# Last rows of a decoder block: final factor, gain and row sum applied by VectorE in place of GpSimd, and one more block of a modulation sum on TensorE

## The chip, the cores and the metric

The kernel runs on one core of one Trainium2 chip. The metric is the device time of one execution in microseconds (us). A core has five engines that run side by side and meet through semaphores: TensorE (PE in the profile, its weight loads PEld), VectorE (DVE), ScalarE (ACT), GpSimd (POOL) and SyncE (SP), which here only issues DMAs.

## What is computed

One layer of a decoder trunk on 512 rows of width 1024, all in float32: an adaLN-modulated RMSNorm, two attention mixers, a gated convolutional MLP, and a final RMSNorm. The two places that the change touches are the first modulation and the last norm:

```python
mod = cs @ w_ada[l] + b_ada[l]                  # cs = silu(c), 1024 long
shift1, scale1, gate1, shift2, scale2, gate2 = jnp.split(mod, 6, axis=-1)
h = _rmsnorm(x, norm1_g[l]) * (1.0 + scale1) + shift1
...
x = x + gate2 * _conv_ffn(h2, ...)
return _rmsnorm(x, final_g)                     # y = x * rsqrt(mean(x*x) + eps) * g
```

## The kernel before, in words

**The whole.** 128 rows or columns make a block. Every fp32 product is made of three matmuls of split values (high times high, high times low, low times high), and TensorE works nearly without a pause from the first projection to the last product. Most of the order of work is written out by hand: inside `tc.manual_schedule` an engine takes its instructions in the order in which the code names them. SyncE's order at the end follows from what it waits for.

**The start.** The first block of columns of the modulation needs two sums over the eight blocks `kk` of `c`: `j = 0` is the scale, `j = 1` the shift. Each is shared between two engines. TensorE multiplies the first `DIRECT[j]` blocks of weights directly with `cs` (`direct0`, L451). VectorE adds the other blocks up in the tile `a0[j]` with one instruction for a block (`add_a0`, L445 for the first, L447 for each further one), and TensorE then sums `a0[j]` over its partitions with a matrix of ones and adds it to the same bank (L475). `finish_mod` (L333 scale, L339 shift) makes the factors, `h_tile` (L383, ScalarE) applies them to the transposed `x` in bank `xt`, and with that the first projection matmul (L403) can run. `turn(t)` (L432) puts the block of rows `t` of `x` into that bank. A float32 matmul appears as two entries ("passes") in the profile, a transpose as one.

**The end.** The last two blocks of rows, 2 and 3 (`u = 0, 1`), get their last product in `last_rows`: all 512 columns of `u = 0`, then columns 0 to 255 (`c0`) and 256 to 511 (`c1`) of `u = 1`, the last piece into a bank of its own (`dX`). From there on only the other engines work. The first half of the 1024 output columns is still to be finished: `last_mul` (L1883) multiplies the bank by the gate, `last_sum` (L1886) adds it to `x`, `last_square` (L1891, ScalarE) squares it and sums each row, `root` (L1903) takes the root, `root_inverse` (L1908, L1910) inverts it, and `rstd_end` (L201, L205) refines it into the row factor `rs`. Meanwhile GpSimd multiplies the new `x` by the final gain `fgb` into `m1` (`last_gain`, L1895; the profile calls the tile `pairs`), and VectorE multiplies that by `rs` (`last_scale`, L1914). The second half of the columns already holds `x` times gain in `e2` (the profile's `chain_outl`) and needs only `rs` (`last_scale2`: VectorE, L1922, for `u = 0`; ScalarE, L1920, for `u = 1`). Each piece is sent out with its own DMA: `u = 0` in two pieces of 256 KB, `u = 1` in four of 128 KB, seven of the eight output DMAs on SyncE's queue (`finished` at L1943 sends rows 0 and 1) and one on ScalarE's.

Of the kernel before, what the change touches and what calls it, by code (L numbers as in the profile page):

```python
# [10 lines left out]
AF = mybir.ActivationFunctionType  # L11
ALU = mybir.AluOpType
PSUM = bass.MemoryType.PSUM

P = 128
D = 1024
S = 512
KT = D // P
# [42 lines left out]
def kernel(  # L61
# [22 lines left out]
    nc = tc.nc  # L84
    xd, wada, win, wout, wup, wdown = x[0], w_ada[0], w_in[0], w_out[0], w_up[0], w_down[0]
    wba, wbd, od = w_branch_swa[0], w_branch_diff[0], out[0]

    def pool(name, bufs=1, space=None, stack=ctx):
        kw = {} if space is None else {"space": space}
        return stack.enter_context(tc.tile_pool(name=name, bufs=bufs, reuse_waits="tile", **kw))  # L90
# [107 lines left out]
    def rstd_end(dst, ms, r0, n, wpool):  # L198
        t = wpool.tile([P, n], F32, tag="rs_b", bufs=3, name="rt")
        if n == 1:  # L200
            nc.vector.scalar_tensor_tensor(t, r0, r0, ms, ALU.mult, ALU.mult)  # L201
        else:
            nc.vector.tensor_mul(t, r0, r0)
            nc.vector.tensor_mul(t, t, ms)
        nc.vector.scalar_tensor_tensor(dst, t, -3.0, r0, ALU.add, ALU.mult)  # L205
# [124 lines left out]
    def finish_mod(k, pa):  # L330
        pa = pa if k == 0 else [pa[:, 0], pa[:, 1]]
        m = pp.tile([P, 16], F32, tag="mod", bufs=3, name=f"mod{k}")
        last = nc.vector.scalar_tensor_tensor(  # L333
            m[:, 0:1], pa[0][:, 0:1], bsc1[:, k : k + 1], n1g[:, k : k + 1], ALU.add, ALU.mult
        )
        if k:
            nc.scalar.activation(m[:, 1:2], pa[1][:, 0:1], AF.Identity, bias=bsh[:, k : k + 1])
        else:
            nc.vector.tensor_add(m[:, 1:2], pa[1][:, 0:1], bsh[:, k : k + 1])  # L339
        mods[k] = m  # L340
        return last
# [12 lines left out]
    def split_hi(k, part=None):  # L354
        if part != 1:
            pl, nb = (wp, WB) if k % 2 == 0 else (pp, 2)
            wh = pl.tile([P, 768], F32R, tag="whi", bufs=nb, name=f"w0h{k}")
            wl = pl.tile([P, 768], F32R, tag="wlo", bufs=nb, name=f"w0l{k}")
            wts[k] = (wh, wl)
            rq, wq, lq = w0_views(k)  # L360
            nc.scalar.copy(wq, rq)
        if part != 0:
            nc.scalar.copy(wts[k][0][:, 512:768], w0[k][:, 512:768])
# [55 lines left out]
    def root(t):  # L419
        rstd_end(rst[:, t : t + 1], *half[t], 1, pp)  # L420
# [10 lines left out]
    def turn(t):  # L431
        nc.tensor.transpose(pts[0][:, t * P : (t + 1) * P], xn[:, t, 0:P], ident)  # L432

    def scale_x(t):
        nc.scalar.activation(xn[:, t, HEAD:], xn[:, t, HEAD:], AF.Copy, scale=rst[:, t : t + 1])

    pa0 = [tbank("pa0", (P, P)), acc6[4][:, :P]]
    a0 = [pp.tile([P, P], F32, name=f"a0_{j}") for j in range(2)]
    DIRECT = (5, 4)

    def add_a0(j, kks):
        for kk in kks:
            w, f = adaw[0][:, j, kk], cs[:, kk : kk + 1]
            if kk == DIRECT[j]:
                nc.vector.tensor_scalar_mul(a0[j], w, f)  # L445
            else:
                nc.vector.scalar_tensor_tensor(a0[j], w, f, a0[j], ALU.mult, ALU.add)  # L447

    def direct0(j):
        for kk in range(DIRECT[j]):  # L450
            nc.tensor.matmul(  # L451
                pa0[j], adaw[0][:, j, kk], cs[:, kk : kk + 1].to_broadcast([P, P]), start=kk == 0, stop=False
            )

    for t in range(NT):
        stat(t)
        if t in (1, 2):
            normalise(t - 1)
            turn(t - 1)
            keep_warm((4, 1)[t - 1])  # L460
    root(2)
    add_a0(0, range(DIRECT[0], KT - 1))
    root(3)
    add_a0(0, range(KT - 1, KT))
    add_a0(1, range(DIRECT[1], KT))
    scale_x(0)
    scale_head(2)
    scale_head(3)
    scale_x(1)
    direct0(0)  # L470
    turn(2)
    direct0(1)
    turn(3)
    for j in range(2):
        nc.tensor.matmul(pa0[j], a0[j], ones, start=False, stop=True)  # L475
    finish_mod(0, pa0)
    split_hi(0, 0)
    keep_warm(2)
# [616 lines left out]
    bp = pool("mlp")  # L1095
# [134 lines left out]
    for h in range(2):  # L1230
        c1 = 2 * P
# [237 lines left out]
    def ks(g):  # L1469
        return slice(2 * (g % 2), 2 * (g % 2) + 2)  # L1470
# [25 lines left out]
    V, q0, q1 = nc.vector, ks(0), ks(1)  # L1496
# [81 lines left out]
    fgb = bp.tile([P, D], F32, tag="fgb", name="fgbr")  # L1578
# [167 lines left out]
    s2 = big.tile([P, NPR, H], F32, tag="hhA", name="s2")  # L1746
# [3 lines left out]
    m1 = pairs2.rearrange("p (t n) -> p t n", n=S)  # L1750
    e = cbuf[1][:, 1024:2048].rearrange("p (t n) -> p t n", n=S)
    e2 = cbuf[3][:, 1024:2048].rearrange("p (t n) -> p t n", n=S)
# [61 lines left out]
    def stat_end(t):  # L1814
        rs = bp.tile([P, 1], F32, tag="rs2", bufs=4, name=f"rsd{t}")
        rstd_end(rs, *parts[t], 1, bp)
        return rs

    def res(t, hf):
        return x1[:, t, hf * S : (hf + 1) * S]  # L1820
# [61 lines left out]
    def last_mul(u, sl=slice(0, S), bank=dW):  # L1882
        nc.vector.tensor_mul(m1[:, u, sl], bank[u][:, sl], gate(0)[:, sl])  # L1883

    def last_sum(u, sl=slice(0, S)):
        nc.vector.tensor_add(res(2 + u, 0)[:, sl], res(2 + u, 0)[:, sl], m1[:, u, sl])  # L1886

    def last_square(u, sl=slice(0, S)):
        sq = big.tile([P, S], F32, tag="sq2", name=f"sqe{u}_{sl.start}")
        s1 = bp.tile([P, 1], F32, tag="ss2", bufs=8, name=f"sse{u}_{sl.start}")  # L1890
        nc.scalar.activation(sq[:, sl], res(2 + u, 0)[:, sl], AF.Square, accum_out=s1)  # L1891
        return s1

    def last_gain(u, sl=slice(0, S)):
        nc.gpsimd.tensor_tensor(m1[:, u, sl], res(2 + u, 0)[:, sl], fgb[:, sl], ALU.mult)  # L1895

    def partial(s1, plus=EPS):
        nc.vector.tensor_scalar(s1, s1, 1.0 / D, plus, ALU.mult, ALU.add)
        return s1
# [3 lines left out]
        nc.scalar.activation(q, s1, AF.Sqrt, bias=plus, scale=1.0 / D)  # L1903
        return q

    def root_inverse(s1, q, plus):
        ms = bp.tile([P, 1], F32, tag="rs_a", bufs=3, name="ms")
        nc.vector.scalar_tensor_tensor(ms, s1, 1.0 / D, plus, ALU.mult, ALU.add)  # L1908
        r0 = bp.tile([P, 1], F32, tag="rs_c", bufs=3, name="r0")
        nc.vector.reciprocal(r0, q)  # L1910
        return ms, r0

    def last_scale(u, rs, sl=slice(0, S)):
        nc.vector.tensor_scalar_mul(res(2 + u, 0)[:, sl], m1[:, u, sl], rs)  # L1914
        nc.sync.dma_start(od[(2 + u) * P : (3 + u) * P, sl], res(2 + u, 0)[:, sl])

    def last_scale2(u, rs, sl=slice(0, S), q=nc.sync):
        dst, src = res(2 + u, 1)[:, sl], e2[:, u, sl]
        if u:
            nc.scalar.activation(dst, src, AF.Copy, scale=rs)  # L1920
        else:
            nc.vector.tensor_scalar_mul(dst, src, rs)  # L1922
        q.dma_start(od[(2 + u) * P : (3 + u) * P, S + sl.start : S + sl.stop], dst)

    def last_rows(todo):
        man = ExitStack()
        man.enter_context(
            tc.manual_schedule(engines={nc.vector.engine, nc.scalar.engine, nc.tensor.engine, nc.gpsimd.engine})
        )
        c0, c1 = slice(0, H), slice(H, S)  # L1930
        part = [partial(parts[2 + u, 1]) for u in range(2)]
        for g in todo:
            multiply(len(passes) - 1, g, 0)

        for g in todo:
            multiply(len(passes) - 1, g, 1, c0)
        for g in todo:
            multiply(len(passes) - 1, g, 1, c1, dX, g == todo[0])
        ends = [stat_end(u) for u in range(2)]

        def finished(u):
            nc.scalar.activation(x1[:, u], x1[:, u], AF.Copy, scale=ends[u])
            nc.sync.dma_start(od[u * P : (u + 1) * P, :], x1[:, u])  # L1943

        finished(0)
        last_mul(0)
        last_sum(0)
        s0 = last_square(0)
        q0 = root(s0, part[0])
        finished(1)  # L1950
        last_gain(0)
        last_mul(1)
        h0 = root_inverse(s0, q0, part[0])
        last_sum(1)
        s1 = last_square(1, c0)
        last_gain(1, c0)
        rs0 = bp.tile([P, 1], F32, tag="rs2", bufs=4, name="rse0")
        rstd_end(rs0, *h0, 1, bp)
        last_mul(1, c1, dX)
        last_sum(1, c1)  # L1960
        s2 = last_square(1, c1)
        last_gain(1, c1)
        partial(s1, part[1])
        q1 = root(s2, s1)
        last_scale(0, rs0)
        last_scale2(0, rs0)
        h1 = root_inverse(s2, q1, s1)
        rs1 = bp.tile([P, 1], F32, tag="rs2", bufs=4, name="rse1")
        rstd_end(rs1, *h1, 1, bp)
        for c in (c0, c1):  # L1970
            last_scale(1, rs1, c)
        for c, q in ((c0, nc.sync), (c1, nc.scalar)):
            last_scale2(1, rs1, c, q)
        man.close()

    ops = {}
# [83 lines left out]
```

## Time and profile before

| | |
|---|---|
| median of 3 runs | 686.99 us (686.57 to 687.71) |
| the profiled execution, its own time | 686.37 us |
| its span in the profile | 684.6 us, so 1.8 us lie outside the span |
| TensorE busy | 674.2 us (98% of the span) |
| VectorE, ScalarE, GpSimd busy | 564.6, 383.4, 102.1 us |
| the chain that ended last | TensorE 97%, DMA 1%, VectorE 1% |

In the timeline each row gives the start, the duration, the engine, the line and the operation, the tiles (out<-in) with their sizes, how many instructions are merged (x2), and in brackets how long the engine stood idle before it and who released it. A letter q behind an engine (SPq, ACTq) marks its DMA issues. Times count from the start of the span.

### The profile page before, as it was taken

The page shows a single profiled execution, that of the slowest core. Times are in us where ns is not written, and L with a number is a line of the kernel's source. Part 1 is how long each engine was busy: PE and PEld are TensorE (multiplying, and loading weights), DVE is VectorE, ACT ScalarE, POOL GpSimd, SP SyncE. Part 2 cuts the span into 40 slices and gives each one's busy share as a digit, 9 for nine tenths or more (in the row PEclk, how much of TensorE's full clock was granted, in tenths as well). Part 3 has the DMA queues.
Part 4 walks back from the last instruction along what each step waited for, and adds up shares of the span by engine and source line. Part 5 has one row for each costly group of instructions (what it writes and reads, how often), then busy time and mean ns, then how long its engine had stood idle before and what let it go on. Part 6 is the DMA issues. An engine that isn't in the chain of part 4 may idle for free.

```text
span 684.6 us, 11125 instructions
## 1 busy us (share of the span) xinstructions
PE 674.2 (98%) x4139; PEld 589.3 (86%) x4139; DVE 564.6 (82%) x1076; ACT 383.4 (56%) x687; POOL 102.1 (15%) x122
## 2 busy tenths in 40 slices
PE   8999999999999999999999999999999999999995
PEld 5887887878888888888899999999999998888884
DVE  5999875988796656884689988888888999979997
ACT  6776774546543233324387665565556565656764
POOL 3000000021012012030030210011121003440301
PEclk9999999999999999999999999999999999999998
DMA  9995412565456785669555788777888648995803
GB/s 307 355 302 176 132 62 76 163 165 156 149 150 190 220 255 172 203 175 334 180 101 108 171 207 214 183 168 204 205 208 212 146 169 198 189 205 143 159 0 123
DMA packets 117286, 123.89 MB, mean 181 GB/s; under 512 B 5079, under 2 KB 94456, under 8 KB 117232
## 3 DMA queue, kind: packets, MB, share of 16 engines
q1 hardware_dynamic: 97390, 95.25, 43.5%
q0 software_dynamic: 19648, 27.79, 24.3%
q8 instruction: 32, 0.52, 0.3%
q14 instruction: 22, 0.18, 0.1%
q10 hardware_dynamic: 194, 0.14, 0.1%
HBM read 118.97 MB, written 2.11 MB: 177 GB/s over the span
## 4 chain that ended last, share of the span: by engine, by line
PE 97%; DMA 1%; DVE 1%; SPq 0%; ACT 0%; issue 0%
PE up L1362 32%; PE dc L2004 15%; PE a L403 5%; PE pga L132 2%; PE pga L134 2%; PE pgd L132 2%; PE pgd L133 2%; PE pga L133 2%; PE pgd L134 2%; PE oc L1419 2%; PE oc L1418 2%; PE oc L1422 2%; PE sd L139 1%; PE pq L132 1%; DMA adaw<-in_w_ada_dram 1%; PE pw L132 1%
## 5 line engine op out<-in xcount | busy, mean ns | idle before, releaser
L1362 PE MATMUL up<-t,m_whi 128*128 128x256 f32 x512 | 93.1, 283 | 0.0
L1362 PEld LDWEIGHTS up<-t,m_whi 128*128 128x128 f32 x512 | 79.9, 192 | 0.0
L1362 PE MATMUL up<-t,m_wlo 128*128 128x256 f32 x256 | 72.4, 283 | 0.0
L1362 PE MATMUL up<-bh,p_whi 128*128 128x256 f32 x232 | 65.7, 283 | 0.0
L1362 PE MATMUL up<-bl,p_whi 128*128 128x256 f32 x232 | 65.7, 283 | 0.0
L1362 PE MATMUL up<-bh,p_wlo 128*128 128x256 f32 x232 | 65.7, 283 | 0.0
L952 POOL DMA_DIRECT2D arow<-arow x28 | 22.5, 803 | 245.2 <-DVE sd L821 123.1
L1362 PEld LDWEIGHTS up<-t,m_wlo 128*128 128x128 f32 x256 | 49.2, 192 | 0.0
L1271 POOL DMA_DIRECT2D s<-in_w_up_dram x21 | 27.2, 1371 | 140.9 <-DMA s<-in_w_up_dram 76.2
L1362 PEld LDWEIGHTS up<-bh,p_whi 128*128 128x128 f32 x232 | 44.5, 192 | 0.0
L1362 PEld LDWEIGHTS up<-bl,p_whi 128*128 128x128 f32 x232 | 44.5, 192 | 0.0
L1362 PEld LDWEIGHTS up<-bh,p_wlo 128*128 128x128 f32 x232 | 44.5, 192 | 0.0
L944 DVE SCALAR_TENSOR_TENSOR arow<-ra,cs,arow 128x512 f32<-128x512 f32 x56 | 41.8, 747 | 0.6
L1299 ACT CAST m_whi<-s 128x1024 fp32r<-128x1024 f32 x31 | 32.5, 1047 | 11.1 <-DVE s L1293 7.7
L1303 DVE TENSOR_TENSOR m_wlo<-s,m_whi 128x1024 fp32r<-128x1024 f32 x31 | 37.8, 1218 | 0.0
L1362 PE MATMUL up<-t,p_whi 128*128 128x256 f32 x176 | 32.2, 283 | 0.0
L1362 PEld LDWEIGHTS up<-t,p_whi 128*128 128x128 f32 x176 | 27.5, 192 | 0.0
L816 ACT ACTIVATE sd<-sd,dmx 128x128 f32<-128x128 f32 (+3 forms) x32 | 17.7, 556 | 17.3 <-DVE dmx L806 17.3
L1369 ACT ACTIVATE gT<-a,cv 128x512 f32<-128x512 f32 x22 | 17.7, 814 | 16.9 <-DVE a L1404 15.8
L1299 ACT CAST p_whi<-wa 128x1024 fp32r<-128x1024 f32 x18 | 18.8, 1042 | 12.3 <-PE up L1362 10.5
L1303 DVE TENSOR_TENSOR p_wlo<-wa,p_whi 128x1024 fp32r<-128x1024 f32 x18 | 22.0, 1221 | 3.8 <-ACT p_whi L1299 3.2
L1362 PE MATMUL up<-t,p_wlo 128*128 128x256 f32 x88 | 24.9, 283 | 0.0
(501 smaller groups left out, 2053.9 us busy)
## 6 DMA issues: line engine op xcount, KB each, us to landing
ra<-in_w_ada_dram SPq DMA_DIRECT2D x32, 512.0 KB, 4.9
wa<-in_w_up_dram SPq DMA_DIRECT2D x22, 512.0 KB, 4.9
s<-in_w_up_dram SPq DMA_DIRECT2D x21, 512.0 KB, 4.9
s<-in_w_up_dram POOLq DMA_DIRECT2D x21, 512.0 KB, 6.9
w<-in_w_in_dram SPq DMA_DIRECT2D x12, 512.0 KB, 4.9
a<-in_w_up_dram SPq DMA_DIRECT2D x11, 512.0 KB, 4.8
b<-in_w_down_dram SPq DMA_DIRECT2D x10, 512.0 KB, 4.0
adaw<-in_w_ada_dram SPq DMA_DIRECT2D x8, 512.0 KB, 6.6
```

The lines of the kernel that those rows point to most:

```text
L132: nc.tensor.matmul(o, lh, rh, start=start, stop=False)
L133: nc.tensor.matmul(o, lh, rl, start=False, stop=False)
L134: nc.tensor.matmul(o, ll, rh, start=False, stop=stop)
L403: nc.tensor.matmul(acc6[i], lhs[:, i * P : (i + 1) * P], rhs[k], start=k == 0 and p == 0, stop=last and p == 2)
L816: exp = nc.scalar.activation(pm[m], pm[m], AF.Exp, bias=mx[:, m : m + 1], scale=slope, accum_out=ls)
L944: nc.vector.scalar_tensor_tensor(ac, r[:, a], cc, ac, ALU.mult, ALU.add)
L952: nc.gpsimd.dma_start(whole[0:n], whole[n : 2 * n], accum_op=ALU.add)
L1271: nc.gpsimd.dma_start(dst, upblock(*blk), accum_op=ALU.add)
L1299: nc.scalar.copy(W[J, name][0], R[J, SRC[name]])
L1303: nc.vector.tensor_sub(lo, R[J, SRC[name]], hi.bitcast(F32))
L1362: nc.tensor.matmul(o[u], w[:, k, cu], b[:, k], start=name in ("p1", "m5", "p2") and k == 0 and x == 0, stop=k == 3 and x == 2, skip_group_ ...
L2004: nc.tensor.matmul(bank2[u][:, sl], a[:, q, cu], b[:, q, sl], start=first_mm and x == 0, stop=last_mm and x == 2, skip_group_check=name no ...
```

## The change

At the start both sums now give TensorE five blocks, and VectorE adds three for the shift where it added four. The transpose of the last block of rows of `x` (`turn(3)`) now stands behind the two matmuls that add `a0`, not ahead of them.

At the end GpSimd's multiplication by the gain is gone. VectorE's `scale_first` applies row factor and gain in one instruction of two tensors and one factor, in place. `last_sum(1)` is cut into `c0` and `c1`, with the reciprocal of `u = 0` between the two. The second half of the columns is scaled by ScalarE for both blocks: for `u = 0` in two pieces, one ahead of the last square and one behind the last root, for `u = 1` in one piece of 512. The second halves go out as one DMA each, `u = 1` on ScalarE's queue, so that there are seven output DMAs.

```diff
-    DIRECT = (5, 4)
+    DIRECT = 5
...
     direct0(0)
     turn(2)
     direct0(1)
-    turn(3)
     for j in range(2):
         nc.tensor.matmul(pa0[j], a0[j], ones, start=False, stop=True)
+    turn(3)
     finish_mod(0, pa0)
...
-    def last_gain(u, sl=slice(0, S)):
-        nc.gpsimd.tensor_tensor(m1[:, u, sl], res(2 + u, 0)[:, sl], fgb[:, sl], ALU.mult)
...
+    def scale_first(u, rs, sl=slice(0, S)):
+        x = res(2 + u, 0)[:, sl]
+        nc.vector.scalar_tensor_tensor(x, x, rs, fgb[:, sl], ALU.mult, ALU.mult)
+        nc.sync.dma_start(od[(2 + u) * P : (3 + u) * P, sl], x)
+
+    def scale_second(u, rs, sl=slice(0, S)):
+        nc.scalar.activation(res(2 + u, 1)[:, sl], e2[:, u, sl], AF.Copy, scale=rs)
+
+    def send_second(u, q):
+        q.dma_start(od[(2 + u) * P : (3 + u) * P, S:], res(2 + u, 1))
...
         finished(1)
-        last_gain(0)
         last_mul(1)
-        h0 = root_inverse(s0, q0, part[0])
-        last_sum(1)
+        ms0 = mean(s0, part[0])
+        last_sum(1, c0)
         s1 = last_square(1, c0)
-        last_gain(1, c0)
+        r0 = inverse(q0)
+        last_sum(1, c1)
         rs0 = bp.tile([P, 1], F32, tag="rs2", bufs=4, name="rse0")
-        rstd_end(rs0, *h0, 1, bp)
+        rstd_end(rs0, ms0, r0, 1, bp)
         last_mul(1, c1, dX)
         last_sum(1, c1)
+        scale_second(0, rs0, c0)
         s2 = last_square(1, c1)
-        last_gain(1, c1)
         partial(s1, part[1])
         q1 = root(s2, s1)
-        last_scale(0, rs0)
-        last_scale2(0, rs0)
-        h1 = root_inverse(s2, q1, s1)
+        scale_first(0, rs0)
+        scale_second(0, rs0, c1)
+        send_second(0, nc.sync)
+        ms1 = mean(s2, s1)
         rs1 = bp.tile([P, 1], F32, tag="rs2", bufs=4, name="rse1")
-        rstd_end(rs1, *h1, 1, bp)
+        rstd_end(rs1, ms1, inverse(q1), 1, bp)
         for c in (c0, c1):
-            last_scale(1, rs1, c)
-        for c, q in ((c0, nc.sync), (c1, nc.scalar)):
-            last_scale2(1, rs1, c, q)
+            scale_first(1, rs1, c)
+        scale_second(1, rs1)
+        send_second(1, nc.scalar)
```

`mean` and `inverse` are the two halves of the old `root_inverse`. Lines that start with a minus are of the kernel before, with a plus of the changed one.

TensorE at the start, from the scale's direct matmuls (`pa`) over the shift's (`a_111`) to the warm-up matmul that follows; `xt` is the bank of transposed `x`:

```order
 L451 MATMUL pa_206<-cs,adaw_130 128x128 x5
 L432 MATMUL xt_205<-ident,xn 128x128
-L451 MATMUL a_111<-cs,adaw_130 128x128 x4
+L451 MATMUL a_111<-cs,adaw_130 128x128 x5
+L474 MATMUL pa_206<-ones,a_0_207 128x128
+L474 MATMUL a_111<-ones,a_1_208 128x128
 L432 MATMUL xt_205<-ident,xn 128x128
-L475 MATMUL pa_206<-ones,a_0_207 128x128
-L475 MATMUL a_111<-ones,a_1_208 128x128
 L184 MATMUL a_113<-ones 128x256
```

The shift gets a fifth direct matmul, and the last transpose has moved behind both sums of `a0`.

VectorE at the end, between the gate multiplication of `u = 1` and that of its last piece; `ms`, `r`, `rt` and `rse` are the steps of the row factor of `u = 0`:

```order
-L1908 SCALAR_TENSOR_TENSOR ms<-sse_0_7145,ssd_7022 128x1
-L1910 RECIPROCAL r_7155<-root 128x1
-L1886 TENSOR_TENSOR x_3151<-x_3151,pairs_3623 128x512
-L201 SCALAR_TENSOR_TENSOR rt<-r_7155,ms 128x1
-L205 SCALAR_TENSOR_TENSOR rse_7162<-rt,r_7155 128x1
+L1905 SCALAR_TENSOR_TENSOR ms<-sse_0_7145,ssd_7022 128x1
+L1886 TENSOR_TENSOR x_3151<-x_3151,pairs_3623 128x256
+L1910 RECIPROCAL r_7158<-root 128x1
+L1886 TENSOR_TENSOR x_3151<-x_3151,pairs_3623 128x256
+L201 SCALAR_TENSOR_TENSOR rt<-r_7158,ms 128x1
+L205 SCALAR_TENSOR_TENSOR rse_7161<-rt,r_7158 128x1
```

The addition of 512 columns has become two of 256 with the reciprocal between them.

VectorE a little later, from the last piece's addition to the reciprocal of `u = 1`:

```order
 L1886 TENSOR_TENSOR x_3151<-x_3151,pairs_3623 128x256
-L1898 TENSOR_SCALAR sse_0_7159<-sse_0_7159,ssd_7026 128x1
-L1914 TENSOR_SCALAR x_3151<-pairs_3623,rse_7162 128x512
-L1922 TENSOR_SCALAR x_3151<-chain_outl,rse_7162 128x512
-L1908 SCALAR_TENSOR_TENSOR ms<-sse_256_7169,sse_0_7159 128x1
+L1895 TENSOR_SCALAR sse_0_7156<-sse_0_7156,ssd_7026 128x1
+L1915 SCALAR_TENSOR_TENSOR x_3151<-x_3151,rse_7161,fgbr 128x512
+L1905 SCALAR_TENSOR_TENSOR ms<-sse_256_7169,sse_0_7156 128x1
 L1910 RECIPROCAL r_7181<-root 128x1
```

Where two passes of 512 columns stood ahead of the factor of `u = 1`, there is now one, and it reads two tensors.

More of the change, by code (lines that the diff above doesn't have):

```diff
@@ L443, in add_a0 @@
             w, f = adaw[0][:, j, kk], cs[:, kk : kk + 1]
-            if kk == DIRECT[j]:
+            if kk == DIRECT:
                 nc.vector.tensor_scalar_mul(a0[j], w, f)
@@ L449, in direct0 @@
     def direct0(j):
-        for kk in range(DIRECT[j]):
+        for kk in range(DIRECT):
             nc.tensor.matmul(
@@ L461 @@
     root(2)
-    add_a0(0, range(DIRECT[0], KT - 1))
+    add_a0(0, range(DIRECT, DIRECT + 2))
     root(3)
-    add_a0(0, range(KT - 1, KT))
-    add_a0(1, range(DIRECT[1], KT))
+    add_a0(0, range(DIRECT + 2, KT))
+    add_a0(1, range(DIRECT, KT))
     scale_x(0)
@@ L1904, in root, with mean, inverse @@
         return q
-    def root_inverse(s1, q, plus):
+    def mean(s1, plus):
         ms = bp.tile([P, 1], F32, tag="rs_a", bufs=3, name="ms")
         nc.vector.scalar_tensor_tensor(ms, s1, 1.0 / D, plus, ALU.mult, ALU.add)
+        return ms
+    def inverse(q):
         r0 = bp.tile([P, 1], F32, tag="rs_c", bufs=3, name="r0")
         nc.vector.reciprocal(r0, q)
[L1911 to L1923, printed above, removed]
+        return r0
+    def scale_first(u, rs, sl=slice(0, S)):
[6 more added lines that the diff above has]
+        q.dma_start(od[(2 + u) * P : (3 + u) * P, S:], res(2 + u, 1))
     def last_rows(todo):
```

## The prediction

> **What bounds the kernel now.** First the page's head and busy times, then the waits of TensorE over the whole body, then the timelines of the two ends.
>
> ```profile
> span 684.6 us, 11125 instructions
> PE 674.2 (98%) x4139; PEld 589.3 (86%) x4139; DVE 564.6 (82%) x1076; ACT 383.4 (56%) x687; POOL 102.1 (15%) x122
> ```
>
> ```profile
> PE xt L432 <- DVE xn L424: 0.3, 1, 0.3
> PE a L403 <- ACT hThA L383: 0.2, 1, 0.2
> ```
>
> The last two rows are the whole list of TensorE's waits from 10 to 672 us: none is later than its first projection matmul (L403), at 15.38. So the body is TensorE's own stream; a shift of its start passes to its end, and what follows the last matmul counts in full. The change touches just these two.
>
> **The start.** In the timeline:
>
> ```profile
> 12.32 0.29 DVE L445 TENSOR_SCALAR a<-adaw,cs 128x128 f32<-128x128 f32 x1
> 12.34 1.16 PE L451 MATMUL a<-cs,adaw 128*128 128x128 f32 x8
> 12.64 1.13 DVE L447 SCALAR_TENSOR_TENSOR a<-adaw,cs,a 128x128 f32<-128x128 f32 x3
> 13.34 0.27 PE L432 MATMUL xt<-ident,xn 128*128 128x128 f32 x1
> 13.45 0.39 PE L475 MATMUL pa<-ones,a 128*128 128x128 f32 x2
> 13.82 0.49 PE L475 MATMUL a<-ones,a 128*128 128x128 f32 x2
> 14.35 0.16 DVE L339 TENSOR_TENSOR mod<-a,cols 128x1 f32<-128x1 f32 x1 [0.26 <-PE a L475]
> 14.54 0.78 ACT L383 ACTIVATE hThA<-xt,mod 128x512 fp32r<-128x512 f32 x1 [0.66 <-DVE mod L339]
> ```
>
> VectorE ends the shift's sum at 12.64 + 1.13 = 13.77; TensorE's last pair waits for it and starts at 13.82; its end (14.31) releases L339, that releases ScalarE, and that the projection.
> - Removed: one of three L447, 1.13 / 3 = 0.38. VectorE is done at 13.39.
> - Added: two passes on TensorE at the 0.11 between the rows at 13.34 and 13.45, 0.22.
> - New order: TensorE is through its direct passes at 13.34 + 0.22 = 13.56, through the scale's pair at 13.78, and starts the shift's pair there; its operand has been ready for 0.39. Without the stall the pair takes 0.39 (row 13.45), not 0.49, and ends at 14.17. The bottleneck changes hands, from VectorE to TensorE, so that of 0.38 only **0.14** is left.
> - Moved: `turn(3)` starts at 13.78 + 0.22 = 14.00 and ends at 14.27. ScalarE needs it as well as L339, now done at 14.21 + 0.16 = 14.37; cover 0.10. Were the cover gone, the start would lose what exceeds it. No DMA moves here.
>
> **The end.** VectorE's rows from the last full bank on, ScalarE's, GpSimd's and the DMA issues:
>
> ```profile
> 674.62 0.69 DVE L1883 TENSOR_TENSOR pairs<-dc,g2b 128x512 f32<-128x512 f32 x1 [0.38 <-PE dc L2004]
> 675.23 0.40 DVE L1908 SCALAR_TENSOR_TENSOR ms<-sse,ssd 128x1 f32<-128x1 f32 x1
> 676.22 0.21 DVE L201 SCALAR_TENSOR_TENSOR rt<-r,ms 128x1 f32<-128x1 f32 x1
> 676.46 0.65 DVE L205 SCALAR_TENSOR_TENSOR rse<-rt,r 128x1 f32<-128x1 f32 x1
> 677.04 0.41 DVE L1883 TENSOR_TENSOR pairs<-dc,g2b 128x256 f32<-128x256 f32 x1
> 677.48 0.43 DVE L1886 TENSOR_TENSOR x<-x,pairs 128x256 f32<-128x256 f32 x1
> 677.95 0.48 DVE L1914 TENSOR_SCALAR x<-pairs,rse 128x512 f32<-128x512 f32 x1
> 678.34 0.95 DVE L1922 TENSOR_SCALAR x<-chain_outl,rse 128x512 f32<-128x512 f32 x1
> 679.21 0.15 DVE L1908 SCALAR_TENSOR_TENSOR ms<-sse,sse 128x1 f32<-128x1 f32 x1
> 679.28 0.15 DVE L1910 RECIPROCAL r<-root 128x1 f32<-128x1 f32 x1
> 679.72 0.16 DVE L205 SCALAR_TENSOR_TENSOR rse<-rt,r 128x1 f32<-128x1 f32 x1
> ...
> 676.40 0.40 ACT L1891 ACTIVATE sqe<-x 128x256 f32<-128x256 f32 x1
> 678.00 0.42 ACT L1891 ACTIVATE sqe<-x 128x256 f32<-128x256 f32 x1 [1.11 <-DVE x L1886]
> 678.59 0.29 ACT L1903 ACTIVATE root<-sse,sse 128x1 f32<-128x1 f32 x1
> 679.91 0.91 ACT L1920 ACTIVATE x<-chain_outl,rse 128x256 f32<-128x256 f32 x2 [1.02 <-DVE rse L205]
> ...
> 674.33 1.29 POOL L1895 TENSOR_TENSOR pairs<-x,fgbr 128x512 f32<-128x512 f32 x1 [11.94 <-DVE x L1886]
> 676.38 0.72 POOL L1895 TENSOR_TENSOR pairs<-x,fgbr 128x256 f32<-128x256 f32 x1 [0.76 <-DVE x L1886]
> 677.99 1.02 POOL L1895 TENSOR_TENSOR pairs<-x,fgbr 128x256 f32<-128x256 f32 x1 [0.89 <-DVE x L1886]
> ...
> 680.37 0.81 SPq L1915 DMA_DIRECT2D out_dram<-x  x2
> 681.27 0.41 SPq L1923 DMA_DIRECT2D out_dram<-x  x1
> ```
>
> The reader is to see three stretched VectorE rows, each beside a GpSimd pass. The same `ms` takes 0.40 and 0.15, the same `rse` 0.65 and 0.16; the first `ms` ends at 675.63, GpSimd's pass at 675.62; the first `rse` at 677.11, the pass at 677.10.
>
> Step by step, without GpSimd:
> - `ms` 675.23 + 0.15 = 675.38. The addition in two pieces of 0.43 (row 677.48), the reciprocal between them hidden by overlaps of 0.07: 676.21. That is 0.09 earlier than the one of 512 ended (L201 follows it at 676.22, with that overlap). `rt`, then `rse` 0.24 behind it, end at 676.54, not 677.11.
> - The last piece's multiplication starts at 676.46 instead of 677.04, 0.58 earlier, so its addition ends at 677.33 and ScalarE's square can start at 677.42. ScalarE's new pass, `scale_second(0, c0)`, 0.5 long (0.91 for two that overlap), stands ahead of that square, behind the square of `c0` that ends at 676.80: it ends at 677.30. Cover 0.12; past that it would delay square, root and factor one for one. The root ends at 678.59 + 0.29 - 0.58 = 678.30.
> - VectorE meanwhile does one pass of two tensors. Its price isn't in these rows; the nearest are
>
> ```profile
> L944 DVE SCALAR_TENSOR_TENSOR arow<-ra,cs,arow 128x512 f32<-128x512 f32 x56 | 41.8, 747 | 0.6
> L300 DVE SCALAR_TENSOR_TENSOR ac<-adaw,cs,ac 128x256 f32<-128x256 f32 x40 | 16.7, 479 | 0.1
> ```
>
>   I take 0.75 and 0.48, the same form and sizes; bounds are 0.48 (L1914) and 0.95 (L1922) for 512. It runs from 677.38 to 678.13, inside the wait for the root; at 0.95 it would still end at 678.33.
> - Reciprocal at 678.33, and to the factor's end 0.60 as before (679.28 to 679.88): 678.93, **0.95 earlier**.
> - `u = 1`: two passes of 0.48 that overlap by 0.08 end at 679.45 and 679.86; SyncE issues at 679.48 and 679.89. ScalarE's 512 in one takes between 0.50, one of the two 256, and 0.91, both: 0.70 taken, issue at 679.69. The last issue moves from 681.27 to 679.89, 1.38 earlier. `send_second(0)` is issued near 678.75 and has left SyncE before 679.48.
>
> [...]
>
> Are 1.38 kept? Here are the output writes:
>
> ```profile
> 681.20:682.90 1.70, 0.00 (x0) 0.00 (x0) 0.00 (x0) 0.00 (x0) 0.00 (x0) 0.50 0.89 309
> 681.75:682.00 0.25, 0.00 (x0) 0.00 (x0) 0.00 (x0) 0.00 (x0) 0.00 (x0) 0.50 1.04 373
> 675.75:677.25 1.50, 0.63 (x6) 0.43 (x4) 1.47 (x4) 1.14 (x3) 0.72 (x1) 1.00 0.01 0
> ```
>
> The last column is GB/s, the one before it the DMA engines' share. 309 GB/s over 1.70 us are the 525 KB of `u = 1`; the writes start 0.83 after their first issue (680.37) and run at 373 GB/s when full, 1.41 us in all. Now they start at 679.48 + 0.83 = 680.31 and, back to back, end near 681.72, against some 682.85: **1.12**. So 0.26 is given back to the queue of writes. What lies behind (landing, SyncE's closing waits) I leave alone; the waits' order may cost or save 0.15.
>
> **Sum.** 0.14 + 1.12 = 1.26 us, 685.1 for the profiled execution (686.37). That one lies 0.6 under the median; against the median it is **685.7**. 0.2%, about what a measurement of this kernel can tell from no change, is 1.37 us: the forecast is just inside.
>
> **The rivals.**
> 1. *The writes don't queue.* Then the last issue's whole 1.38 counts: 0.14 + 1.38, 685.5. For: a share of 0.89 leaves gaps. Against: 1.04 at full flow.
> 2. *The start's gain is lost*, if `turn(3)` or the loads behind the projection take over: 685.9. Against: covers of 0.10 and 0.39, and no later wait of TensorE.
> 3. *Slower: GpSimd is not what stretches VectorE.* If something else at this place does (DMA writes, ScalarE), `ms` and `rse` stay at 0.40 and 0.65, and the heavier passes stretch as L1922 did, 0.95 to 0.48: 512 takes 1.48, 677.95 to 679.43; `ms` to 679.75; reciprocal, `rt` and `rse` to 680.65; two pieces of 0.95 to 682.5; last issue at 682.5, and its 128 KB are written by 683.7 instead of 682.85. With the start's 0.14 that is 687.7. It decides once the 512 pass ends later than 678.30 + 0.95. Against: the writes stand still in the last quoted row while `rse` takes 0.65, and L1914 keeps 0.48 in full flow until GpSimd starts at 677.99. [...]
>
> **How the numbers follow.** Forecast 0.62 (about 45 in 100 of it beyond 1.37 us, given the runs' scatter of 1.1: 0.28 faster, 0.34 same); rival 1 0.20, faster; rival 2 0.06, same; rival 3 0.12, of which 0.09 beyond 0.2% with what it may add. Faster 0.48, same 0.43, slower 0.09. The range goes from rival 1 less half the scatter, 685.0, to the forecast plus what the runs spread, 686.8; rival 3 is left out.
>
> **What would show it.** Right: no GpSimd row near the end; `ms` 0.15 and `rse` 0.16 both times; `rse` of `u = 1` about 0.95 nearer to the last matmul; L1915 at 0.75; writes full for 1.4 us; L383 at 14.40, released by L339. Wrong: L383 released by the transpose; ScalarE's square waiting for its own queue; a stretched VectorE row without GpSimd; a DMA wait of TensorE after 15 us.

## The result and the profile after

| | before | after |
|---|---|---|
| median of 22 runs each, taken side by side | 686.76 us | 685.68 us |
| ratio, with its 95% interval | | 0.9984 (0.9977 to 0.9991) |
| profiled execution, own time | 686.37 us | 685.90 us |
| its span | 684.6 us | 684.1 us |

The change saves 1.08 us, 0.16%, by an interval clear of zero; 685.7 was forecast. The two profiled executions differ by 0.47 us only, so the gain can't be read from their spans. Two stretches of the trace can be compared instead, as they end and begin at the same instructions: the **start**, from the shift's first direct matmul (L451) to the first projection matmul (L403), and the **tail**, from VectorE's multiplication of the last full bank (L1883, its second row) to the end of the span.

The start after the change, TensorE's, VectorE's and ScalarE's rows of the timeline (three dots stand for rows that are left out):

```profile
12.41 1.38 PE L451 MATMUL a<-cs,adaw 128*128 128x128 f32 x10
13.63 0.39 PE L474 MATMUL pa<-ones,a 128*128 128x128 f32 x2
13.85 0.39 PE L474 MATMUL a<-ones,a 128*128 128x128 f32 x2
14.08 0.27 PE L432 MATMUL xt<-ident,xn 128*128 128x128 f32 x1
...
15.36 0.50 PE L403 MATMUL a<-hThA,w0h 128*128 128x512 f32 x1
...
14.28 0.16 DVE L339 TENSOR_TENSOR mod<-a,cols 128x1 f32<-128x1 f32 x1
...
14.53 0.78 ACT L383 ACTIVATE hThA<-xt,mod 128x512 fp32r<-128x512 f32 x1 [0.59 <-DVE mod L339]
```

TensorE's two pairs now follow its direct matmuls without a stall, and L339 still releases ScalarE. The start takes 15.36 - 12.41 = 2.95 us, where it took 3.04.

The tail after the change: VectorE, ScalarE, and the DMA issues:

```profile
675.17 0.69 DVE L1883 TENSOR_TENSOR pairs<-dc,g2b 128x512 f32<-128x512 f32 x1 [0.38 <-PE dc L2004]
675.78 0.15 DVE L1905 SCALAR_TENSOR_TENSOR ms<-sse,ssd 128x1 f32<-128x1 f32 x1
...
676.89 0.16 DVE L205 SCALAR_TENSOR_TENSOR rse<-rt,r 128x1 f32<-128x1 f32 x1
...
677.89 0.74 DVE L1915 SCALAR_TENSOR_TENSOR x<-x,rse,fgbr 128x512 f32<-128x512 f32 x1
...
678.87 0.16 DVE L1910 RECIPROCAL r<-root 128x1 f32<-128x1 f32 x1 [0.16 <-ACT root L1900]
...
679.32 0.16 DVE L205 SCALAR_TENSOR_TENSOR rse<-rt,r 128x1 f32<-128x1 f32 x1
679.51 0.88 DVE L1915 SCALAR_TENSOR_TENSOR x<-x,rse,fgbr 128x256 f32<-128x256 f32 x2
...
677.35 0.49 ACT L1919 ACTIVATE x<-chain_outl,rse 128x256 f32<-128x256 f32 x1
677.95 0.42 ACT L1891 ACTIVATE sqe<-x 128x256 f32<-128x256 f32 x1
...
678.54 0.30 ACT L1900 ACTIVATE root<-sse,sse 128x1 f32<-128x1 f32 x1
...
679.51 0.72 ACT L1919 ACTIVATE x<-chain_outl,rse 128x512 f32<-128x512 f32 x1 [0.28 <-DVE rse L205]
680.26 0.38 ACTq L1922 DMA_DIRECT2D out_dram<-x  x1
...
680.02 0.83 SPq L1916 DMA_DIRECT2D out_dram<-x  x2
```

No row is stretched any more. VectorE waits 0.16 for the root: the fused pass of 512, 0.74, is done before. The factor of `u = 1` is ready 679.48 - 675.17 = 4.31 after the tail's start, where it took 5.26 (679.88 - 674.62), and the tail lasts 8.93 to the span's end, where it took 9.94.

So the two stretches give 0.09 + 1.01 = 1.10 us, which agrees with the medians. Why the profiled spans hide over half of it is seen in a row of ScalarE's, the first of these three, after the change:

```profile
49.20 1.05 ACT L128 CAST w_h<-w 128x1024 fp32r<-128x1024 f32 x1 [0.57 <-DMA w<-in_w_in_dram]
50.15 0.25 ACT L337 ACTIVATE mod<-pa,cols 128x1 f32<-128x1 f32 x1
50.44 0.78 ACT L383 ACTIVATE hThB<-xt,mod 128x512 fp32r<-128x512 f32 x1
```

and in TensorE's only wait from 10 to 672 us there:

```profile
PE a L403 <- ACT hThB L383: 0.2, 1, 0.2
```

In that execution a weight load came late. The cast that waited for it stood ahead of the last column block's factors on ScalarE, and from the first L403 to the last it took 39.97 us instead of 39.41 before. The runs below decide whether that belongs to the change.

### The profile page after: what moved, and what is told of

It is laid out like the page before. It is cut to its first block, busy times and chain, and to the rows that moved or that the text cites. A ratio compares the mean times of both kernels' runs of the same rounds, so it can differ in the third digit from the quotient of the medians.

```text
span 684.1 us, 11125 instructions
## 1 busy us (share of the span) xinstructions
PE 675.3 (99%) x4141; PEld 589.7 (86%) x4141; DVE 564.2 (82%) x1075; ACT 384.5 (56%) x688; POOL 98.5 (14%) x119
```

## The experiments

Eleven kernels were run on the chip, and the changed one was profiled twice. Their starts and tails, with the time where it was taken in several rounds:

| kernel | start | tail | median, and before beside it | ratio (95% interval) |
|---|---|---|---|---|
| before | 3.04 | 9.94 | | |
| after | 2.95 | 8.93 | 685.68, 686.76 | 0.9984 (0.9977 to 0.9991) |
| start alone | 2.95 | 9.94 | 686.28, 686.48 | 0.9996 (0.9988 to 1.0005) |
| end alone | 3.03 | 8.93 | 685.36, 686.48 | 0.9983 (0.9971 to 0.9996) |
| before, no GpSimd passes | 3.04 | 8.95 | 686.14, 686.48 | 0.9996 (0.9983 to 1.0009) |
| after, GpSimd passes back | 2.95 | 9.94 | 686.26, 686.48 | 0.9998 (0.9989 to 1.0007) |
| after, one tensor | 2.95 | 8.83 | | |
| after, less sent | 2.95 | 8.43 | | |
| after, transpose early | 3.00 | 8.93 | | |
| after, finer pieces | 2.95 | 9.02 | 685.54, 686.91 | 0.9984 (0.9975 to 0.9993) |
| after, no refining steps | 2.95 | 8.68 | 685.18, 686.31 | 0.9986 (0.9977 to 0.9995) |
| after, once more | 3.19 | 8.94 | 685.76, 686.31 | 0.9990 (0.9981 to 1.0000) |

The stretches repeat to 0.01 or 0.02 us (but for the last start, told below), while single runs of one kernel spread by more than 1 us. Effects of 0.1 us are read from the stretches alone.

**The start alone and the end alone.** The edits are the two halves of the diff.

> The kernel before with the start of the changed one alone (five direct blocks for both sums, last transpose behind). From the shift's first direct matmul (L451) to the first projection matmul (L403) it took 3.04 us before and 2.95 in the changed kernel; from VectorE's multiplication of the full bank (L1883, second row) to the span's end 9.94 and 8.93. Theory (the start gives its share alone): 2.95 and 9.94, the time 0.1 us below before, too little to tell by the times alone. Rival (the start's gain is lost to loads behind the projection): 2.95 there, but TensorE is as late as before at 60 us, and the changed kernel's late load at 49 us is seen here as well, since starting earlier is what provokes it.

> The changed kernel with the start of before. Theory (the end gives nearly all): 3.04 us from L451 to L403, 8.93 us from the full bank's multiplication to the span's end, the time 1.0 us below before (ratio 0.9985). Rival (half of it is the start's): 0.5 us below before. If the late load at 49 us in the changed kernel's profile belongs to its earlier start, it is absent here; if it is chance, it can be there or not.

Both came out: 2.95 and 9.94, 3.03 and 8.93. The halves add up. TensorE waited nowhere from 10 to 672 us in the start alone, and the late load was in neither profile (39.56 and 39.54 us from the first L403 to the last), so this half of the rival for the start fell.

The other half, that TensorE is as late as before at 60 us, stays open. From the shift's first direct matmul to the last L403 it is 2.95 + 39.56 = 42.51 us in the start alone, 3.04 + 39.41 = 42.45 in the kernel before and 3.03 + 39.54 = 42.57 in the end alone. The two profiles with the old start differ by more than the 0.09 that the new one wins, and the time (0.20 below before, with an interval on both sides of zero) can't tell either. That the 0.09 reaches the end of the kernel is not shown.

**GpSimd's passes taken out of before.**

```diff
-        last_gain(0)
...
-        last_gain(1, c0)
...
-        last_gain(1, c1)
...
     def last_scale(u, rs, sl=slice(0, S)):
-        nc.vector.tensor_scalar_mul(res(2 + u, 0)[:, sl], m1[:, u, sl], rs)
+        nc.vector.tensor_scalar_mul(res(2 + u, 0)[:, sl], res(2 + u, 0)[:, sl], rs)
```

> The kernel before without GpSimd's three passes; nothing takes their place, so that the final gain is left out of the first half of the last two blocks of rows. Theory (GpSimd stretches VectorE): the first ms 0.15 instead of 0.40 us, the first rse 0.16 instead of 0.65, the pass of L1922 0.48 instead of 0.95, and 9.0 us from the full bank's multiplication to the span's end instead of 9.94. Rival (something else stretches them): 0.40, 0.65 and 0.95 stay, and 9.9.

VectorE's rows there (L1905, L205 and L1919 are the old L1908, L205 and L1922):

```profile
678.55 0.15 DVE L1905 SCALAR_TENSOR_TENSOR ms<-sse,ssd 128x1 f32<-128x1 f32 x1
...
679.72 0.16 DVE L205 SCALAR_TENSOR_TENSOR rse<-rt,r 128x1 f32<-128x1 f32 x1
...
681.11 0.48 DVE L1919 TENSOR_SCALAR x<-chain_outl,rse 128x512 f32<-128x512 f32 x1
```

All three fell to their short form, and the tail to 8.95. That is 0.99 of the 1.01 that the whole change brings there, with the old order, the old eight DMAs and nothing fused. The times show less, 0.34, but can't be read that finely: the profiled execution (span 686.9) lost some 2.5 us, as TensorE waited 2.9 us for the split of a weight in the middle of the kernel, and another was as long, of which there is no trace.

**GpSimd's passes put back beside the changed end.**

```diff
+    def idle_gain(u, sl=slice(0, S)):
+        nc.gpsimd.tensor_tensor(m1[:, u, sl], res(2 + u, 0)[:, sl], fgb[:, sl], ALU.mult)
```

It is called at the three old places; nobody reads the result.

> The changed kernel with GpSimd's three multiplications back in their places, into the old tile that nobody reads any more. Theory (GpSimd stretches VectorE): the first ms 0.40 us, the first rse 0.65, the fused pass of 512 up to 1.2 beside the third GpSimd pass, and 9.5 to 10.0 us from the full bank's multiplication to the span's end instead of 8.93, so that most of the gain is gone. Rival (the gain is from the shorter order of work, not from GpSimd's absence): 0.15, 0.16, 0.75 and 8.9.

The whole gain of the end was gone: 9.94. VectorE's rows, then GpSimd's:

```profile
674.82 0.41 DVE L1908 SCALAR_TENSOR_TENSOR ms<-sse,ssd 128x1 f32<-128x1 f32 x1
...
675.56 0.40 DVE L1886 TENSOR_TENSOR x<-x,pairs 128x256 f32<-128x256 f32 x1
675.89 0.68 DVE L201 SCALAR_TENSOR_TENSOR rt<-r,ms 128x1 f32<-128x1 f32 x1
...
677.59 0.74 DVE L1918 SCALAR_TENSOR_TENSOR x<-x,rse,fgbr 128x512 f32<-128x512 f32 x1
678.25 0.68 DVE L1908 SCALAR_TENSOR_TENSOR ms<-sse,sse 128x1 f32<-128x1 f32 x1
...
673.91 1.30 POOL L1895 TENSOR_TENSOR pairs<-x,fgbr 128x512 f32<-128x512 f32 x1 [11.92 <-DVE x L1886]
675.64 0.90 POOL L1895 TENSOR_TENSOR pairs<-x,fgbr 128x256 f32<-128x256 f32 x1 [0.43 <-DVE r L1913]
677.63 1.29 POOL L1895 TENSOR_TENSOR pairs<-x,fgbr 128x256 f32<-128x256 f32 x1 [1.08 <-DVE x L1886]
```

Two expectations missed in detail. `rt` was stretched (0.68) and not `rse` (0.16), as `rt` now met GpSimd's second pass. And the fused pass of 512, begun 0.04 ahead of GpSimd's third pass, kept its 0.74, and GpSimd's pass took 1.29; in the kernel before the two passes of this size took 0.72 and 1.02. Then VectorE's next small step ended with it, at 678.93 against 678.92. In these rows the one that began first kept the time it takes in the changed kernel, without GpSimd (the fused pass 0.74 in both, the second L1886 0.40 and 0.41), and the small VectorE step that began behind GpSimd's pass ended with it (`rt` at 676.57, the pass at 676.54). So it was in the kernel before: L1914, begun at 677.95, was 0.04 ahead of GpSimd's pass and kept its 0.48 beside it (0.47 in the run without GpSimd's passes), which the prediction had put down to the time before GpSimd's start. Not every row waits: L1883, begun 0.29 inside GpSimd's first pass in the kernel before (674.62 against 674.33), kept the 0.69 that it takes without GpSimd. What sets it apart is not shown.

**What the fused pass costs.**

```diff
-        nc.vector.scalar_tensor_tensor(x, x, rs, fgb[:, sl], ALU.mult, ALU.mult)
+        nc.vector.tensor_scalar_mul(x, x, rs)
```

> The changed kernel with the row factor alone in scale_first, one tensor instead of two; the final gain is left out of the first half of the last two blocks of rows. What the fusing costs on the path: 512 columns 0.48 instead of 0.75 us, hidden by the wait for the root, and 256 columns 0.35 instead of 0.48. Counted from the multiplication of the full bank: factor of u = 1 still at 4.31, first issue of the last block's data 0.13 earlier, the writes' end 7.05 to 7.1 instead of 7.20, the span's end 8.8 instead of 8.93. Rival (the writes of u = 0 ahead in the queue set the end): 8.93.

8.83: fusing costs 0.10 on the path. The two pieces took 0.62 together instead of 0.88, the first issue came 0.13 earlier, but the last write only 0.05; the other 0.05 came behind the last write, where no reason is shown.

**Fewer bytes in the last DMA.** Of `u = 1`'s second half 64 columns are sent instead of 512.

```diff
-        q.dma_start(od[(2 + u) * P : (3 + u) * P, S:], res(2 + u, 1))
+        w = D if u == 0 else S + 64
+        q.dma_start(od[(2 + u) * P : (3 + u) * P, S:w], res(2 + u, 1)[:, : w - S])
```

> The changed kernel with 64 of the 512 columns sent in the last DMA on ScalarE's queue, 32 KB instead of 256; the rest of the last block's second half is left unwritten. All is computed and issued as before. Theory (the last writes run back to back, so that bytes set the end): the writes' end moves from 7.20 us after the full bank's multiplication to about 6.6, the time of the last issue's own piece, and the span's end from 8.93 to 8.3. Rival (the last issue sets the end whatever is queued): 7.2 and 8.9.

The output writes in quarters of a microsecond (the last two columns are the DMA engines' share and GB/s), first where the changed kernel stops writing, then where this one does:

```profile
681.50:681.75 0.25, 0.00 (x0) 0.00 (x0) 0.00 (x0) 0.00 (x0) 0.00 (x0) 1.00 1.03 401
...
682.00:682.25 0.25, 0.00 (x0) 0.00 (x0) 0.00 (x0) 0.00 (x0) 0.00 (x0) 0.50 1.01 352
682.25:682.50 0.25, 0.00 (x0) 0.00 (x0) 0.00 (x0) 0.00 (x0) 0.00 (x0) 0.50 0.11 33
```

```profile
680.75:681.00 0.25, 0.00 (x0) 0.00 (x0) 0.00 (x0) 0.00 (x0) 0.00 (x0) 0.50 1.00 352
681.00:681.25 0.25, 0.00 (x0) 0.00 (x0) 0.00 (x0) 0.00 (x0) 0.00 (x0) 0.50 0.09 25
```

Counted from the tail's start (675.17 and 674.41), the last write is done at 7.20 and at 6.70, with all issues where they were. Both ends came 0.1 later than expected, and the tail shrank by 0.50. So in the changed kernel the bytes in the queue set the end, not the last issue.

**The transpose back ahead of the sums.**

```diff
     direct0(1)
+    turn(3)
     for j in range(2):
         nc.tensor.matmul(pa0[j], a0[j], ones, start=False, stop=True)
-    turn(3)
```

> The changed kernel with the last transpose back ahead of the two sums at the start. From L451 to L403 it took 2.95 us with the transpose behind, 3.04 in the kernel before. Theory (TensorE's stream sets the start now, and ScalarE pays 0.06 for waiting on two engines at once): the shift's factor comes 0.11 later, for the transpose's place, and ScalarE starts 0.035 behind it instead of 0.095: 3.00. Rival (the transpose behind the sums is what ScalarE waits for): 2.90 or less, better than the change.

3.00, as the theory had it. In the timeline of this kernel L339 starts at 14.08 and ScalarE's L383 at 14.27:

```profile
14.08 0.16 DVE L339 TENSOR_TENSOR mod<-a,cols 128x1 f32<-128x1 f32 x1
14.27 0.78 ACT L383 ACTIVATE hThA<-xt,mod 128x512 fp32r<-128x512 f32 x1 [0.47 <-DVE mod L339]
```

From L339's end to ScalarE it is 0.03 here, 14.53 - 14.44 = 0.09 in the changed kernel, though the transpose had ended at 14.35. Moving the transpose wins its 0.11 on TensorE and gives back 0.06 on ScalarE.

What stands between L339's end and ScalarE's start is in the trace of the changed kernel. Among ScalarE's instructions of L383 it has one on a semaphore, of 17 ns:

```profile
L383 ACTq EVENT_SEMAPHORE  x1: 17/17/17, 14.5 to 14.5; - x1
```

It stands at 14.47, 0.03 behind L339's end, and the activation follows 0.06 behind it. The kernel before, with the transpose ahead of the sums, has no such row in its start, and its activation starts 0.03 behind L339 (14.54 - 14.51), as it does in this run. What the row waits for is not shown. The transpose as such is not what comes late: where the changed kernel's trace has ScalarE released by transposes (L835, which end at 200.26, ahead of L536), it starts 0.04 behind them, not the 14.53 - 14.35 = 0.18 found here.

**Two further versions.** Finer pieces at the end, and `u = 0`'s second half in two DMAs (`send_second` takes the columns now):

```diff
         scale_second(0, rs0, c0)
+        send_second(0, nc.sync, c0)
...
-        send_second(0, nc.sync)
+        send_second(0, nc.sync, c1)
...
-        for c in (c0, c1):
+        for c in (slice(0, P), slice(P, H), c1):
             scale_first(1, rs1, c)
-        scale_second(1, rs1)
-        send_second(1, nc.scalar)
+        for c in (c0, c1):
+            scale_second(1, rs1, c)
+            send_second(1, nc.scalar, c)
```

> The changed kernel with finer pieces at the end: the first 256 columns of the last block's first half in two passes and DMAs of 128, the second half of both blocks in two DMAs of 256 columns, that of u = 0 sent as soon as its first piece is scaled. If the writes' first byte and then their bandwidth set the end: first issue 0.13 us earlier, and the writes' end at 7.0 to 7.1 instead of 7.20, the span's end 8.75 to 8.85 instead of 8.93, the time 0.1 us below the changed kernel and 1.2 below before. If more DMAs cost more in issues than finer pieces bring: 8.95 to 9.2.

The tail grew to 9.02. ScalarE's second piece stood behind its own DMA issue (idle 0.45), so the last issue came at 679.94 - 674.10 = 5.84 into the tail, where the changed kernel's came at 5.28. The rival with more issues was right by the tail; 0.09 us is too little for the times (685.54 beside 686.91) to show.

```profile
679.40 0.51 ACT L1919 ACTIVATE x<-chain_outl,rse 128x256 f32<-128x256 f32 x1 [0.45 <-ACT x L1919]
679.94 0.37 ACTq L1922 DMA_DIRECT2D out_dram<-x  x1
```

Without the refining steps of the last block's factor, and with `u = 0`'s first second-half piece sent early. `rstd_end` makes (r * r * ms - 3) * r of the inverted root r, close to -2 * r when r * r * ms is close to 1, and the edit takes -2 * r itself:

```diff
         scale_second(0, rs0, c0)
+        send_second(0, nc.sync, c0)
...
-        send_second(0, nc.sync)
-        ms1 = mean(s2, s1)
+        send_second(0, nc.sync, c1)
...
-        rstd_end(rs1, ms1, inverse(q1), 1, bp)
+        nc.vector.tensor_scalar_mul(rs1, inverse(q1), -2.0)
```

> The changed kernel with two steps of the last block's factor taken out: its row factor is the reciprocal of the root times minus two, without the refining steps L201 and L205, and the first piece of u = 0's second half is sent as soon as it is scaled, so that the queue is free earlier. If the last block's first issue and then the bytes set the end: factor of u = 1 at 4.05 to 4.1 us after the full bank's multiplication instead of 4.31, the writes' end at about 7.0 instead of 7.20, the span's end 8.7 instead of 8.93, the time 0.2 below the changed kernel. If u = 0's writes still stand in the queue: 8.9.

8.68, as expected: 0.25 below the changed kernel, from both edits together. The times, 685.18 beside its 685.76, differ by more than that; medians of runs that spread by over 1 us can't be read to 0.3. Its factor rests on ScalarE's root alone for one block; what that costs in exactness was not measured.

**The changed kernel once more.**

> The changed kernel as it is, beside the version without the refining steps. The segments repeat: 2.95 us from L451 to L403, 8.93 from the full bank's multiplication to the span's end, time 1.1 us below before. Whether the late load at 49 us of its first profile is chance: theory, chance, absent here, and 39.5 us from the first L403 to the last as in the other profiles instead of 39.97. Rival, its own: 39.9 again.

From the first L403 to the last it took 39.49 us, and in the nine other profiles between 39.49 and 39.73, seven of them with the new start. So nothing ties the late load to the change. The expectation of 1.1 us below before missed: 685.76 beside 686.31 is 0.55, with an interval (0.9981 to 1.0000) that holds both this and the 0.9984 of the 22 runs. The start of this profile, 3.19, is another accident: TensorE waited twice for L424's `xn`, 2.7 us in all, and its granted clock was 0.50 from 12 to 14 us.

```profile
11.18 0.33 PE L432 MATMUL xt<-ident,xn 128*128 128x128 f32 x1 [1.53 <-DVE xn L424]
...
12.00:14.00 2.00, 2.00 (x10) 2.00 (x11) 1.72 (x7) 1.69 (x4) 0.33 (x1) 0.50 1.09 366
```

## Why the prediction was right, and where it was off

**The time.** The forecast of 685.7 and the 685.68 measured agree better than the sum does, and by luck: 1.26 us were forecast and 1.08 measured, 0.18 less, and the kernel before came out at 686.76 over 22 runs, 0.23 below the 686.99 of three runs from which the forecast had started. The two nearly cancel. The stretches are the fairer comparison: 1.26 forecast, 1.10 found. The saving is 0.16%, so it stayed below the prediction's own mark of 0.2% (a chance of 0.43 was given to that) and did not pass it (0.48).

**Start.** Forecast 0.14, measured 0.09. The handover from VectorE to TensorE was as worked out: L339 ended 0.14 earlier after L451. What was mis-sized is the moved transpose: it was costed at nothing, with a cover of 0.10 in time. The cover held, and ScalarE still started 0.06 later behind L339, behind the semaphore instruction that the prediction did not reckon with. That the 0.09 lasts to the end of the kernel was taken from the list of TensorE's waits and is not shown.

**Tail up to the last issue.** The steps were right to 0.04 us or so: factor of `u = 1` forecast 4.31 after the tail's start (678.93 - 674.62) and found there; first issue 4.86 and 4.85, last issue 5.27 and 5.28 (680.45, behind the first one on SyncE). The fused pass of 512 took 0.74 where 0.75 was taken, the second half's 512 on ScalarE 0.72 where 0.70 was.

**Writes.** That 1.38 would not be kept was right, and the run with fewer bytes shows the reason. The writes' end was forecast at 7.10 into the tail and found at 7.20. What was mis-sized is their rate. `u = 1`'s writes were to start 0.83 behind their first issue (680.02, so at 680.85) and to take 1.41 at 373 GB/s; the trace has 346 GB/s from there to their end:

```profile
680.85:682.37 1.52, 0.00 (x0) 0.00 (x0) 0.00 (x0) 0.00 (x0) 0.00 (x0) 0.82 0.95 346
```

The 373 were one quarter of a microsecond of the kernel before, and the rate at full share here is now 401, now 352. Before, the end was at 8.26: 1.06 gained, not 1.12.

**Behind the writes.** Left alone in the forecast; it took 1.73 instead of 1.68. That and the writes leave 1.01.

**The account of causes** was less exact than the sum. The prediction followed the new order step by step and let it all appear as one gain. The two GpSimd runs show that the passes' absence is worth 0.99 to 1.01 and everything else at the end, taken together, some 0.02: what the new order, ScalarE's relief of VectorE and the merged DMA bring (8.95 - 8.83 = 0.12, the two kernels without the gain), the fused pass takes back (0.10). Rival 3 is refuted by the same two runs, and rival 1 by the run with fewer bytes and by the 1.06 that was kept of 1.38. Rival 2 is not settled: the loads behind the start are not seen to take over, but the profiles scatter by more than the 0.09 in question.

## What to carry to other kernels

Where two engines may hold each other up, as VectorE and GpSimd do in the rows here, look in the timeline for the same small instruction at two durations (`rse` 0.65 and 0.16). Here its long form ended with the other engine's pass (677.11 and 677.10), and the price of giving work away was the wait of what stood on the path at that moment (0.99 of the tail), not the work saved. Behind the last matmul count the output's bytes against its first issue before shortening the issues: here 64 columns in the last DMA instead of 512 took 0.50 off the tail, with all issues where they were. And when a change is worth less than the runs' scatter, measure the stretch between two instructions that both versions have: here it repeats to 0.02 us where the time scatters by 1.

## What the runs showed of the hardware that was not expected

GpSimd's passes were held up beside VectorE's rows, as VectorE's rows were beside GpSimd's. Three of its passes of 256 columns, which read 1.02, 0.90 and 1.29 us, all take 0.58 or 0.59 when counted from the end of the VectorE row that had begun first: 679.01 - 678.43 in the kernel before (behind L1914), 676.54 - 675.96 and 678.92 - 678.33 with the passes put back (behind L1886 and the fused pass). So these three read as waits for the whole of that row. The fourth, 0.72 in the kernel before, takes 0.67 when counted from the end of `rt` (677.10 - 676.43), and no pass of this size in these rows runs without a VectorE row beside it.

In the changed kernel's start ScalarE's activation L383 has a semaphore instruction of its own ahead of it (14.47, 0.03 behind L339's end) and starts 0.06 us behind that (14.53); in the kernel before it has none there and starts 0.03 behind L339's end.

In the last profile two waits of TensorE between the matmuls of L184, 1.2 and 1.5 us, were followed by a stretch at a granted clock of 0.50 (12 to 14 us; 1.00 in the changed kernel's first profile), and the start, which begins behind them, took 0.24 us more. One profile shows this, and no run varied the pauses.
